# The third group of seven products moves to the last gate and up stage, and steps of sums are asked for at other places

## The chip, the cores and the metric

The kernel runs on one core of a Trainium2 chip. The metric is the time of one execution on the device in microseconds; the time before is 1002.94 us, the median of three runs (1001.95 to 1003.80).

## The reference, cut to what matters

Two layers over x of 256 positions by 1024 features, in float32. Each layer adds half a gated feed-forward, then a token mixer, then half of a second feed-forward:

```python
def swiglu(h, w_gate_up, w_down):
    a, b = jnp.split(h @ w_gate_up, 2, axis=-1)
    return (jax.nn.silu(a) * b) @ w_down

def hybrid_layer(x, ...):
    x = x + 0.5 * swiglu(rms_norm(x, ffn1_norm), ffn1_w_gate_up, ffn1_w_down)
    z = rms_norm(x, mix_norm) @ w_in
    u, q, k, v, gl = z[..., :o1], z[..., o1:o2], z[..., o2:o3], z[..., o3:o4], z[..., o4:]
    y_pool = multiscale_pool(u, pool_w, pool_scale)
    q = rope(rms_norm(q, q_norm)); k = rope(rms_norm(k, k_norm))
    y_attn = moba_attention(q, k, v)
    gates = jax.nn.sigmoid(gl + b_gate)
    x = x + (gates[0] * (y_pool @ w_branch_pool) + gates[1] * (y_attn @ w_branch_attn)) @ w_out
    x = x + 0.5 * swiglu(rms_norm(x, ffn2_norm), ffn2_w_gate_up, ffn2_w_down)
    return x
```

D is 1024, the feed-forward is 2816 wide (22 blocks of 128), and the mixer has 8 heads of 64. With 256 positions there is a single block of keys, so attention is causal within it.

## The kernel before, in words

**Units.** All weights lie in DRAM as units of 128 x 2048 float32, 1 MB each. `fetch` (line 143) has SyncE load one into a `raw` buffer (4 of them); ScalarE rounds it to `hi` (line 209) and VectorE takes the rest as `lo` (line 210), in two halves each. There is room for three units in parts, and `ahead` keeps what is split but not yet used. TensorE multiplies the parts with the parts of x (`hx`), all from the one helper at line 110. `plan` is the fixed order of the units.

**Stages.** The program runs six stages: layer 0's first feed-forward, its mix, its second feed-forward (base `FU`), layer 1's first (`LU`), its mix, and its second (`LU + FU`), the last. A feed-forward has a gate and up part (22 blocks), and a down part, whose 8 output columns are added to x.

**Groups in seven forms.** In the last three feed-forwards some of the blocks are not computed as wide pairs (`pair`, 32 matmuls each, one unit) but in groups of four blocks, by Strassen's and Winograd's scheme: seven products (`seven`, 16 matmuls each, one unit each) of forms of x and forms of the weights, and two turns (`turned`, four transposes each). Forms 1, 2 and 3 are quadrants of the weights; forms 4, 5, 6 and 7 are sums of quadrants. `FEED` says for each base which table gives the order: `TWO` has groups A and C (14 wide pairs, 14 products), `THREE` has A, B and C (10 wide pairs, 21 products). The forms of x (`x_forms`) are made at the head of each stage: all at once in `TWO`, one per entry of the table in `THREE`.

**Steps of sums.** The sums of quadrants are made ahead of time by DMAs from DRAM to DRAM, eight steps a group, 56 in all: a copy (`f7`, `f5` from the weights, `f6` from `f7`, `f4` from `f6`), and an accumulating DMA behind it. `far_sums` lists them in order, and each call of `go_on` has GpSimd issue the next one (line 183), behind the VectorE operation that was last marked when the call was made. An accumulating step waits for its copy to land, and a copy of a sum waits for that sum. GpSimd's queue is in order, so whatever stands behind a waiting step waits too; the only other work there is `pool_sums`, the pooling of the mix (lines 857 to 862), whose result VectorE reads in `pool_diff` (line 868), and one memset per mix (line 810). All DMAs share the 16 DMA engines: the loads go by SyncE's queue, the steps by GpSimd's.

**The end.** `add_x` ends each column of the down part. With `late_r` the factor r of the normalisation is applied to the column there (lines 674 to 676, and 681 and 682 for the very last column); without it, it has been applied to gate and up (line 468 in place of 465), and the last column needs line 684 alone. `late_r` is off in the last stage if that stage uses `TWO`.

Of the kernel before, what the change touches and what calls it, by code (L numbers as in the profile page):

```python
# [44 lines left out]
FU = NF + NF // 2 + 24  # L45
LU = FU + NF + NF // 2
# [7 lines left out]
TWO = (0, 1, "1A", 2, "2A", 3, 4, "7A", 5, "6A", 6, "5A", 7, "4A", "3A", 8, "t1A", "1C", (9, "t0A"), "2C", 10, "7C", 11, "6C",  # L54
       16, "5C", 17, "4C", "3C")
THREE = (0, 1, "1A", 2, "2A", "1B", 3, 4, "7A", "6A", 5, "5A", 6, "4A", "2B", "3A", "7B", "6B", 7, "t0A", "t1A", "5B",
         16, "1C", "4B", "3B", "6C", (17, "t0B"), "7C", "t1B", "5C", "2C", "3C", "4C")
FEED = {FU: TWO, LU: THREE, LU + FU: TWO}


def groups_of(base):
    return "AC" if FEED[base] is TWO else "ABC"


def feed_units(base):

    for n in FEED[base]:
        n = n[0] if isinstance(n, tuple) else n
# [6 lines left out]
C_G1, C_GM, C_G2, C_BG, C_PS, NG = 0, 8, 16, 24, 40, 44  # L75
# [3 lines left out]
def trunk_kernel(ctx: ExitStack, tc: tile.TileContext, x_in, w_in, pw_in, qkn_in, rope_in, mask_in, band_in, out):  # L79
    nc = tc.nc  # L80
# [47 lines left out]
    def unit():  # L128

        if not ahead:  # L130
            fetch()
        return ahead.pop(0)
# [17 lines left out]
    far, steps_left = {}, []  # L150

    def quadrant(base, g, q):

        n, kh = base + GROUPS[g] + (0 if q[1] == "1" else 2), int(q[0]) - 1
        return w_in[n:n + 2, :, kh * HALF:(kh + 1) * HALF].rearrange("u p c -> p u c")

    def two_rows(z):
        return z.rearrange("p (i c) -> p i c", i=2)

    def far_sums():  # L160

        rest = []
        for base in STAGES:
            for g in groups_of(base):
                one, two = ({z[0]: (base, g, z[0], z[i], kw) for z in SUMS}
                            for i, kw in ((1, {}), (2, {"accum_op": OP.add})))
                for z in one["7"], one["5"], two["7"]:
                    steps_left.append(z)
                    steps_left.extend(rest[:1])
                    rest = rest[1:]  # L170
                steps_left.extend((two["5"], one["6"]))
                rest = [two["6"], one["4"], two["4"]]
        steps_left.extend(rest)

    def go_on():

        if not steps_left:
            return
        base, g, f, src, kw = steps_left.pop(0)
        if not kw:  # L180
            far[f, g, base] = far_pool.tile([P, 2 * HALF], F32, name="f" + f, tag=f"{base}{g}{f}")
        src = two_rows(far[src, g, base]) if len(src) == 1 else quadrant(base, g, src)
        z = nc.gpsimd.dma_start(two_rows(far[f, g, base]), src, **kw)  # L183
        tc.add_manual_dep(z.ins, marks[-1].ins.name, mybir.DependencyInfo(
            mybir.DependencyClass.Sync, mybir.DependencyReason.DATA), reason="behind")
# [60 lines left out]
    def pair(w, t, other=None, at=0):  # L246

        ps = banks(pmm, "ps")
        columns(w, ps, range(at))
        if other:  # L250
            other()
        columns(w, ps, range(at, NK))
        drain(t, ps)
# [34 lines left out]
    x = gx[:, L * NG:L * NG + NK * S].rearrange("p (k s) -> p k s", s=S)  # L288
# [18 lines left out]
    for t in range(PAD - 1):  # L307
        g = min(g for g, w in enumerate(WINDOWS) if t < w - 1)
# [7 lines left out]
    def split_x(f, l, col):  # L316

        g = gain[:, l, col + f:col + f + 1]
        act(hx[:, f, 0, :], x[:, f, :], AF.Copy, scale=g)
        stt(hx[:, f, 1, :], x[:, f, :], g, hx[:, f, 0, :].bitcast(F32), op0=OP.mult, op1=OP.subtract)  # L320

    def square_x(f):

        if f == 0:
            act(acc, x[:, f, :], AF.Square)
        else:
            sq = small.tile([P, S], F32, name="sq", tag="sq", bufs=2)
            act(sq, x[:, f, :], AF.Square)
            tt(acc, acc, sq, op=OP.add)

    def prep(f, l, col):
        split_x(f, l, col)
        square_x(f)
# [83 lines left out]
    def bc2(a):  # L417
        return a.unsqueeze(1).to_broadcast([P, 2, a.shape[-1]])

    def ffn(after, n0=0, end=False, col=None, base=0, far_at=(), steps_at=()):  # L420
# [15 lines left out]
        abs_, more = {}, []  # L436
        late_r = not (end and FEED[base] is TWO)
        last = {}
# [38 lines left out]
        if n0:  # L477
# [6 lines left out]
            for i in range(n0 + 1, NF + 1):  # L484
                if i < NF:
                    pair(unit(), wide(i))
                    fetch()
                    if i >= 8 and i % 2 == 0:
                        go_on()
                if i == NF or i % 3 != 1:  # L490
                    for n in range(done, NF if i == NF else min(done + 2, i - 1), 2):
                        scaled = post(n)
                        done = n + 2
                        if i == n0 + 1:
                            behind(scaled, drained[-1])
        else:
# [11 lines left out]
            vt = acts.tile([P, 2, GW], F32, name="vt", tag="v")  # L508
            three = FEED[base] is THREE
            tk = {g: acts.tile([P, 2, GW], F32, name="tk", tag="tok", bufs=2) for g in ("AB" if three else "AC")}  # L510
# [113 lines left out]
            if three:  # L624
                go_on()
            for n in FEED[base][2:]:
                next(xf, None)
# [74 lines left out]
    def normed(pt, rt, name):  # L702
        z = acts.tile([P, 2, GW], F32, name=name, **({"tag": "v"} if name == "v" else {"tag": "tok", "bufs": 2}))
        for t in range(2):
            act(z[:, t, :], pt[:, t], AF.Copy, scale=rt[:, t:t + 1])
        return z
# [87 lines left out]
    def mix(l, after):  # L794
# [5 lines left out]
        pt = tokens()  # L800
        r = spread(*z)
        k = normed(pt, rt, "k")
        spare = acts.tile([P, 8 * GW], F32, name="spare", tag="ga")
        yk, pk = ([z[:, i] for i in range(4)] for z in (
            acts.tile([P, 4, 2, S], F32R, name=n, tag=t) for n, t in (("yk", "gc"), ("pk", "gd"))))
# [23 lines left out]
        def project_u():  # L829
            us = [unit() for _ in range(2)]  # L830
            for g in range(0, NW, 2):
                ps = banks(pmm, "ps")
                for k in range(NK):
                    for j in range(2):
                        chain(ps[:, j], *us[k // 4], k % 4 * 4 + g + j, hk[k], k == 0, k == NK - 1)
                z = uT[:, g:g + 2, PAD:]
                drain(z, ps)
                tt(z, z, bc2(r), op=OP.mult)

        pool = [gates[6 + g // 2][:, g % 2, :] for g in range(NW)]  # L840
        W = PAD + S
# [57 lines left out]
        rest = slice(3 * P, 4 * P)  # L899
# [45 lines left out]
        for h in range(NH):  # L945
            gate(h, *((lambda: score_two(h // 2), NK // 2) if h % 4 == 0 else ()))
            if h == 4:
                for p, y in enumerate(ys):
                    heads_end(p, y)
                known = soften_two()  # L950
            elif h < 2:
                soften(h)
            elif h % 4 == 2:
                turn_two(h // 4 * 2, (0, 1) if h > 4 else ())
            elif h == 3:
                pool_diff()
            open_gate(h)
            for _ in range(2 if h < 3 else 1):
                go_on()

        def branch(f, j, k0=0, k1=4):
# [40 lines left out]
        for f in range(4, NK):  # L1002
            if f % 2 == 0:
                ws.append(unit())
                go_on()
            for j in range(2):
                branch(f, j)
            if f == 5:
                fetch()
            mixed(f)  # L1010
        ws, sums = [], []

        def project(f, k0=0, k1=NK):
            if f % 2 == k0 == 0:
                ws.append(unit())
                go_on()
            if k0 == 0:
                sums.append(quarter("ps"))
            ps = sums[f][:, 0]
            chain3(ps, *ws[f // 2], f % 2 * 8 + k0, mk[k0:k1], k0 == 0, k1 == NK)  # L1020
            if k1 == NK:
                marks.append(tt(x[:, f, :], ps, x[:, f, :], op=OP.add))
                after(f)
# [4 lines left out]
    w3 = [buffers() for _ in range(3)]  # L1028
# [20 lines left out]
    for l in range(L):  # L1049
        l_of[0] = l  # L1050
        if l == 0:
            far_sums()
        ffn(lambda f: prep(f, l, C_GM), len(w3) if l == 0 else 0, col=C_G1, base=l * LU, far_at=(1, 3, 5, 7, 9), steps_at=(2,))
        if l == 0:
            for d, z in ((rope, rope_in), (mask, mask_in), (qkn, qkn_in)):
                nc.sync.dma_start(d, z)
        mix(l, lambda f: prep(f, l, C_G2))
        if l + 1 < L:
            ffn(lambda f: prep(f, l + 1, C_G1), col=C_G2, base=FU, far_at=(1, 3, 5, 7, 9), steps_at=(3, 6, 10, 16))
        else:  # L1060
            ffn(lambda f: nc.sync.dma_start(out[:, f, :], x[:, f, :]), end=True, col=C_G2, base=LU + FU)


# [88 lines left out]
```

## Time and profile before

| | |
|---|---|
| median of three runs | 1002.94 us |
| the profiled execution | 1001.16 us |
| its span, first to last instruction | 999.4 us |
| TensorE busy | 990.3 us (99%) |
| TensorE weight loads | 898.5 us (90%) |
| VectorE busy | 805.5 us (81%) |
| ScalarE busy | 654.9 us (66%) |
| GpSimd busy | 62.7 us (6%) |
| granted TensorE clock | 1.0 |
| moved by DMA | 273.65 MB, mean 274 GB/s |

Busy shares are of the span of one profiled execution; line numbers in the rows are those of the kernel before. In the rows PE is TensorE and PEld its weight loads, DVE is VectorE, ACT ScalarE, POOL GpSimd, and SP SyncE; a small q is the engine's queue. `raw<-w` is a weight load, `raw<-f` the load of a sum, and `f<-w` and `f<-f` are steps. `ps` are the sums of wide pairs, `b` those of products.

### The profile page before, as it was taken

How to read it: one execution, taken by the hardware profiler on the slowest of the kernel's cores; microseconds unless marked ns; L12 is line 12 of the kernel's file. 1: busy time of each engine (PE TensorE's matmuls, PEld its weight loads, DVE VectorE, ACT ScalarE, POOL GpSimd, SP SyncE). 2: the span in 40 equal slices, each digit the busy share in tenths (PEclk: the TensorE clock that was granted, in tenths of full speed). 3: DMA queues.
4: the chain of work that ended last, by engine and by line, in shares of the span. 5: the costliest groups of instructions: out<-in, count | busy, mean ns of one | idle time of the engine just before them, and what ended most of it. 6: DMA issues, size and time to landing. Idle time of an engine off the chain costs nothing.

```text
span 999.4 us, 16133 instructions
## 1 busy us (share of the span) xinstructions
PE 990.3 (99%) x6304; PEld 898.5 (90%) x6304; DVE 805.5 (81%) x1141; ACT 654.9 (66%) x981; POOL 62.7 (6%) x103
## 2 busy tenths in 40 slices
PE   9999999999999989999999999999999999999998
PEld 8988999998899978889898889988988998888898
DVE  6987767698788689887689998876988788988862
ACT  7856555567666587775568877555677568776641
POOL 0000001003101000000000000000130000000000
PEclk9999999999999999999999999999999999999999
DMA  8879899958999989898969989887878665787740
GB/s 295 315 269 274 312 317 266 318 194 252 281 345 313 341 311 318 330 323 331 306 216 297 340 293 324 323 288 247 229 250 296 192 213 211 255 285 260 252 148 22
DMA packets 47756, 273.65 MB, mean 274 GB/s; under 512 B 4576, under 2 KB 5856, under 8 KB 24928
## 3 DMA queue, kind: packets, MB, share of 16 engines
q1 hardware_dynamic: 35808, 213.90, 58.2%
q0 software_dynamic: 11872, 58.72, 23.9%
q8 instruction: 49, 0.80, 0.3%
q14 instruction: 27, 0.22, 0.1%
HBM read 271.56 MB, written 59.77 MB: 332 GB/s over the span
## 4 chain that ended last, share of the span: by engine, by line
PE 94%; DMA 2%; DVE 2%; ACT 1%; issue 0%; SPq 0%; ACTq 0%
PE ps L110 66%; PE b L110 13%; PE pt L110 7%; PE two L110 4%; DMA raw<-w 2%; PE pe L110 1%; PE sc L110 1%; DVE lo L210 1%; PE pt L780 1%; PE y L110 1%; PE b L588 0%; PE tp L736 0%; ACT pre L529 0%; PE pt L588 0%; ACT hi L209 0%
## 5 line engine op out<-in xcount | busy, mean ns | idle before, releaser
L210 DVE TENSOR_TENSOR lo<-raw,hi 128x1024 fp32r<-128x1024 f32 (+2 forms) x311 | 368.4, 1197 | 109.0 <-ACT hi L209 106.7
L209 ACT ACTIVATE hi<-raw 128x1024 fp32r<-128x1024 f32 (+2 forms) x311 | 318.4, 1033 | 202.7 <-PE ps L110 114.7
L110 PE MATMUL ps<-hx,hi 128*128 128x512 f32 x1248 | 423.4, 385 | 2.1 <-DVE ab L259 1.5
L110 PE MATMUL ps<-hx,lo 128*128 128x256 f32 x1248 | 341.8, 274 | 0.0
L110 PEld LDWEIGHTS ps<-hx,hi 128*128 128x128 f32 x1248 | 235.0, 188 | 44.8 <-DVE ab L259 1.8
L110 PEld LDWEIGHTS ps<-hx,lo 128*128 128x128 f32 x1248 | 235.3, 189 | 0.2 <-DVE lo L210 0.2
L199 DVE TENSOR_TENSOR lo<-raw,hi 128x1024 fp32r<-128x1024 f32 x98 | 118.5, 1221 | 26.0 <-ACT hi L198 25.7
L198 ACT ACTIVATE hi<-raw 128x1024 fp32r<-128x1024 f32 x98 | 102.9, 1055 | 49.8 <-PE ps L110 19.3
L110 PE MATMUL ps<-ga,hi 128*128 128x512 f32 (+1 forms) x264 | 87.8, 378 | 0.0
L110 PE MATMUL b<-hi,sf 128*128 128x512 f32 x224 | 76.6, 383 | 0.0
L110 PE MATMUL ps<-ga,lo 128*128 128x256 f32 x256 | 70.0, 273 | 0.0
L183 POOL DMA_DIRECT2D f<-w x42 | 39.3, 981 | 482.8 <-DVE ab L259 219.7
L110 PE MATMUL ps<-gb,hi 128*128 128x512 f32 (+1 forms) x198 | 65.4, 376 | 0.0
L110 PE MATMUL pt<-hi,hx 128*128 128x512 f32 x192 | 64.9, 384 | 0.0
L110 PE MATMUL b<-lo,sf 128*128 128x256 f32 x224 | 61.5, 275 | 2.5 <-DVE lo L199 2.5
L110 PEld LDWEIGHTS ps<-ga,hi 128*128 128x128 f32 x264 | 49.0, 188 | 8.2
L110 PE MATMUL pt<-lo,hx 128*128 128x256 f32 x192 | 52.5, 274 | 0.0
L110 PE MATMUL ps<-gb,lo 128*128 128x256 f32 x192 | 52.4, 273 | 0.0
L110 PE MATMUL b<-hi,hx 128*128 128x512 f32 x168 | 51.8, 388 | 0.0
L110 PEld LDWEIGHTS b<-hi,sf 128*128 128x128 f32 x224 | 42.0, 188 | 7.4
L110 PEld LDWEIGHTS ps<-ga,lo 128*128 128x128 f32 x256 | 48.1, 188 | 0.0
L110 PEld LDWEIGHTS b<-lo,sf 128*128 128x128 f32 x224 | 42.0, 188 | 2.8 <-DVE lo L199 2.8
(214 smaller groups left out, 1577.0 us busy)
## 6 DMA issues: line engine op xcount, KB each, us to landing
raw<-w SPq DMA_DIRECT2D x169, 1024.0 KB, 7.1
f<-w POOLq DMA_DIRECT2D x42, 1024.0 KB, 12.9
raw<-f SPq DMA_DIRECT2D x28, 1024.0 KB, 6.7
raw<-w SPq DMA_DIRECT2D x16, 256.0 KB, 5.4
out_dram<-gx SPq DMA_DIRECT2D x8, 128.0 KB, 1.9
gx<-x SPq DMA_DIRECT2D x3, 256.0 KB, 5.8
qk<-pw SPq DMA_DIRECT2D x2, 256.0 KB, 3.8
gx<-x SPq DMA_DIRECT2D x1, 300.0 KB, 2.9
```

Source lines behind the costliest of these rows:

```text
L110: return keep(nc.tensor.matmul(*args, **kw))
L183: z = nc.gpsimd.dma_start(two_rows(far[f, g, base]), src, **kw)
L198: act(hv, a, AF.Copy)
L199: tt(lv, a, hv.bitcast(F32), op=OP.subtract)
L209: act(hi, w, AF.Copy)
L210: return tt(lo, w, hi.bitcast(F32), op=OP.subtract)
L780: keep(nc.tensor.transpose(pt[:, h, o * P:(o + 1) * P], pr[:, h, c * P:(c + 1) * P], ident))
```

## The change

The table `THREE` goes from `LU` to `LU + FU`, and `TWO` from `LU + FU` to `LU`. `late_r` is thereby on in the last stage. `far_sums` now ends a stage's list before it begins the next one; before, the last three steps of a group were mixed with the first of the next group, across stages too. And `go_on` is called elsewhere:

```diff
-FEED = {FU: TWO, LU: THREE, LU + FU: TWO}
+FEED = {FU: TWO, LU: TWO, LU + FU: THREE}
...
 def far_sums():
-        rest = []
         for base in STAGES:
+            rest = []
             for g in groups_of(base):
...
-        steps_left.extend(rest)
+            steps_left.extend(rest)
...
-                    if i >= 8 and i % 2 == 0:
+                    if i in (8,11,14,17,19,21):
                         go_on()
...
         k = normed(pt, rt, "k")
+        go_on()
...
                 tt(z, z, bc2(r), op=OP.mult)
+                if g in (0,2):
+                    go_on()
...
             open_gate(h)
-            for _ in range(2 if h < 3 else 1):
+            if h in (0,2,3,4,5,6,7):
                 go_on()
...
                 ws.append(unit())
-                go_on()
+                if f in (6,):
+                    go_on()
...
                 ws.append(unit())
-                go_on()
+                if f in (4,):
+                    go_on()
...
-        ffn(..., base=l * LU, far_at=(1, 3, 5, 7, 9), steps_at=(2,))
+        ffn(..., base=l * LU, far_at=(1,3,5,7,9) if l else (1,3,5,7,9), steps_at=(6,11))
...
-            ffn(..., base=FU, far_at=(1, 3, 5, 7, 9), steps_at=(3, 6, 10, 16))
+            ffn(..., base=FU, far_at=(1,3,5,7,9), steps_at=(6,11))
...
-            ffn(..., end=True, col=C_G2, base=LU + FU)
+            ffn(..., end=True, col=C_G2, base=LU + FU, steps_at=(2,))
```

Counted from the code, the 56 steps are asked for so:

| stage | before | now |
|---|---|---|
| layer 0, first feed-forward | 12 | 11 |
| layer 0, mix | 20 | 15 |
| layer 0, second feed-forward (`FU`) | 9 | 7 |
| layer 1, first feed-forward (`LU`) | 7 | 7 |
| layer 1, mix | 8 | 15 |
| layer 1, second feed-forward (`LU + FU`) | 0 | 1 |

In layer 0's mix, 11 of the 20 stood at the gates, two at the branches and four at the output columns; of the 15 now, seven stand at the gates, one at the branches, one at the output columns, and two at the pooling's input.

GpSimd in layer 0's mix, from the last step ahead of the pooling sums on (`gates` and `spare` are written by the sums, `uT` is their input). Before:

```order
L183 DMA f6_1957<-w 256x1x1024
L858 TENSOR_TENSOR gates_2058<-uT_2056 128x256
L857 TENSOR_TENSOR spare_2051<-uT_2056 128x3x271
L857 TENSOR_TENSOR spare_2051<-spare_2051 128x2x269
L858 TENSOR_TENSOR gates_2058<-spare_2051 128x256 x2
```

Now:

```order
L183 DMA f4_2210<-f6_2049 16x16384
L861 TENSOR_TENSOR gates_2058<-uT_2056 128x256
L183 DMA f4_2210<-w 256x1x1024
L183 DMA f7_2316<-w 256x1x1024
L860 TENSOR_TENSOR spare_2051<-uT_2056 128x3x271
L860 TENSOR_TENSOR spare_2051<-spare_2051 128x2x269
L861 TENSOR_TENSOR gates_2058<-spare_2051 128x256 x2
```

Two steps stand between the first of the pooling sums and the others, and the first of them accumulates into the copy issued two rows above it, for whose landing it waits.

GpSimd in layer 1's mix, from the end of the pooling sums to the end of the program. Before:

```order
L862 TENSOR_TENSOR spare_7134<-spare_7134,uT_7139 128x64
L183 DMA f5_6835<-w 256x1x1024
L183 DMA f6_7501<-f7_6631 16x16384
L183 DMA f6_7501<-w 256x1x1024
L183 DMA f4_7566<-f6_7501 16x16384
L183 DMA f4_7566<-w 256x1x1024
```

Now:

```order
L865 TENSOR_TENSOR spare_7103<-spare_7103,uT_7108 128x64
L183 DMA f6_7330<-w 256x1x1024
L183 DMA f5_7600<-w 256x1x1024
L183 DMA f4_7655<-f6_7330 16x16384
L183 DMA f7_7368<-w 256x1x1024
L183 DMA f4_7655<-w 256x1x1024
L183 DMA f5_7600<-w 256x1x1024
L183 DMA f6_7930<-f7_7368 16x16384
L183 DMA f6_7930<-w 256x1x1024
L183 DMA f4_8382<-f6_7930 16x16384
L183 DMA f4_8382<-w 256x1x1024
```

Ten steps stand there in place of five: seven at the gates, one at the branches, one at the output columns, and the last one at the head of the last feed-forward.

SyncE's loads at the head of the last feed-forward (`w` of 128x2048 is a wide pair's unit, 128x2x1024 a quadrant, `f` a sum). Before:

```order
L193 DMA raw_8668<-w 128x2x1024
L143 DMA raw_8694<-w 128x2048
L193 DMA raw_8741<-w 128x2x1024
L143 DMA raw_8789<-w 128x2048
L143 DMA raw_8838<-w 128x2048
L193 DMA raw_8889<-f7_4798 128x2048
L143 DMA raw_8915<-w 128x2048
L193 DMA raw_8960<-f6_6534 128x2048
```

Now:

```order
L193 DMA raw_8648<-w 128x2x1024
L143 DMA raw_8674<-w 128x2048
L193 DMA raw_8721<-w 128x2x1024
L193 DMA raw_8759<-w 128x2x1024
L143 DMA raw_8793<-w 128x2048
L143 DMA raw_8841<-w 128x2048
L193 DMA raw_8896<-f7_5086 128x2048
L193 DMA raw_8922<-f6_6502 128x2048
L143 DMA raw_8948<-w 128x2048
```

A quadrant of the new group and the sum `f6` come earlier, so that two products follow each other without a wide pair between them, twice. Inside a stage of two or of three groups, the orders of TensorE, VectorE and ScalarE are those that such a stage had before.

More of the change, by code (lines that the diff above doesn't have):

```diff
@@ L1052, in trunk_kernel @@
             far_sums()
-        ffn(lambda f: prep(f, l, C_GM), len(w3) if l == 0 else 0, col=C_G1, base=l * LU, far_at=(1, 3, 5, 7, 9), steps_at=(2,))
+        ffn(lambda f: prep(f, l, C_GM), len(w3) if l == 0 else 0, col=C_G1, base=l * LU,
+            far_at=(1,3,5,7,9) if l else (1,3,5,7,9), steps_at=(6,11))
         if l == 0:
@@ L1058, in trunk_kernel @@
         if l + 1 < L:
-            ffn(lambda f: prep(f, l + 1, C_G1), col=C_G2, base=FU, far_at=(1, 3, 5, 7, 9), steps_at=(3, 6, 10, 16))
+            ffn(lambda f: prep(f, l + 1, C_G1), col=C_G2, base=FU, far_at=(1,3,5,7,9), steps_at=(6,11))
         else:
-            ffn(lambda f: nc.sync.dma_start(out[:, f, :], x[:, f, :]), end=True, col=C_G2, base=LU + FU)
+            ffn(lambda f: nc.sync.dma_start(out[:, f, :], x[:, f, :]), end=True, col=C_G2, base=LU + FU, steps_at=(2,))
 def _feat(a):
```

## The prediction, made before the change was run

> **What bounds the kernel now.** I read the page first, then the waits of TensorE, the chain of work, and last the stretches by window. The page's first part says how full each engine is:
>
> ```profile
> span 999.4 us, 16133 instructions
> ...
> PE 990.3 (99%) x6304; PEld 898.5 (90%) x6304; DVE 805.5 (81%) x1141; ACT 654.9 (66%) x981; POOL 62.7 (6%) x103
> ```
>
> TensorE is the bound, 9.1 us idle in a span of 999.4. A matmul busy for longer than it need be would hide in this figure, but the change removes or adds no matmul shape, so only the idle time can move. The waits of TensorE, whole span (waiter, releaser: us in total, times, longest):
>
> ```profile
> PE b L110 <- DVE lo L199: 2.5, 1, 2.5
> PE ps L110 <- DVE ab L259: 1.5, 1, 1.5
> PE busy L110 <- DVE eps L298: 1.1, 1, 1.1
> PE ps L110 <- ACT hi L209: 0.6, 1, 0.6
> ```
>
> The last two are the start of the program. The first two, 4.0 us, are the only waits in the middle, and both lie between 345 and 370 us, the head of layer 0's second feed-forward. The chain of waits shows what they hang on (start, us, what):
>
> ```profile
> 321.89 19.11 DMA raw<-w
> ...
> 341.37 1.06 ACT hi L198
> ...
> 356.68 3.22 ACT pre L529 x8
> ...
> 365.16 1.15 DVE lo L199
> 366.35 1.40 PE b L110 x7
> ```
>
> A 1 MB weight load took 19.11 us; ScalarE and VectorE, which split each load before TensorE can use it, ran late behind it and caught up only at 366. Why it took so long is in the windows of line 183, the steps of sums that GpSimd issues (POOL busy and count, clock, DMA share, GB/s):
>
> ```profile
> 240.00:290.00 50.00, 7.37 (x9) 1.00 0.97 300
> 290.00:345.00 55.00, 6.66 (x8) 1.00 1.03 322
> ...
> 514.00:560.00 46.00, 2.11 (x2) 1.00 0.92 293
> ...
> 735.00:790.00 55.00, 4.17 (x5) 1.00 0.80 249
> 790.00:830.00 40.00, 0.00 (x0) 1.00 0.63 211
> 830.00:870.00 40.00, 0.00 (x0) 1.00 0.64 237
> ```
>
> 17 steps were issued from 240 to 345, and the DMA engines were full. In the run-up to the last feed-forward (790 to 830) there was none. The DMA issues of three windows give the weight load's median landing time, first 290 to 345, then 514 to 560, then 790 to 830:
>
> ```profile
> raw<-w SPq DMA_DIRECT2D x8, 1024.0 KB, 16.1
> raw<-f SPq DMA_DIRECT2D x1, 1024.0 KB, 18.9
> ```
>
> ```profile
> raw<-w SPq DMA_DIRECT2D x6, 1024.0 KB, 7.3
> ```
>
> ```profile
> raw<-w SPq DMA_DIRECT2D x8, 1024.0 KB, 5.1
> ```
>
> So a load takes 5.1 us beside no step, 7.3 beside two, 16.1 beside eight. All busy times by window (PE, PEld, DVE, ACT, POOL, clock, DMA) show what each does to TensorE:
>
> ```profile
> 345.00:370.00 25.00, 20.98 (x124) 18.33 (x124) 22.44 (x35) 22.33 (x34) 0.50 (x1) 1.00 0.84 299
> 514.00:560.00 46.00, 46.00 (x278) 41.30 (x277) 43.61 (x57) 39.76 (x56) 2.11 (x2) 1.00 0.92 293
> ...
> 830.00:870.00 40.00, 40.00 (x242) 35.94 (x241) 38.23 (x51) 33.34 (x47) 0.00 (x0) 1.00 0.64 237
> ```
>
> Of the three heads of sevens, only the one behind the crowded mix leaves TensorE idle (25.00 - 20.98 = 4.0 us). The clock is full throughout.
>
> **The change, part by part.** *The third group moves.* It replaces four wide pairs by seven products and two turns. From the chain (a wide pair, a product, a turn):
>
> ```profile
> 517.58 2.72 PE b L110 x16
> 520.30 5.34 PE ps L110 x32
> ...
> 607.63 0.44 PE b L588 x4
> ```
>
> That is 4 x 5.34 = 21.4 us out and 7 x 2.72 + 2 x 0.44 = 19.9 in: 1.5 us less in the last feed-forward, 1.5 more in layer 1's first. The sum is nothing, as long as both heads stay fed. The order of VectorE, ScalarE and TensorE inside a stage of two or of three groups is unchanged; the last feed-forward now runs what the 514 to 560 row shows, where VectorE is 43.61 of 46.00 busy and TensorE did not wait. It hides the split work by only a little, so its cover is the speed of the loads: rival two prices that.
>
> *The end.* With three groups in the last stage the factor r comes in at line 672 and after, not at line 468. The last column of the output, at 996.08, was one VectorE operation behind the last matmul; now there are two:
>
> ```profile
> 996.08 0.42 DVE L684 SCALAR_TENSOR_TENSOR gx<-ps,gx 128x256 f32<-128x256 f32 x1 [6.19 <-PE ps L110]
> ```
>
> Nothing lies beside it, so it adds 0.4 us to the path. The other seven columns have their operations beside matmuls (the same row shows VectorE idle for 6.19 us): nothing. The halved scaling at line 465 in place of line 468 is VectorE time in the middle, hidden: nothing.
>
> *The steps.* Of line 183, over the span:
>
> ```profile
> L183 POOL DMA_DIRECT2D f<-w x42: 672/1049/1544, 59.4 to 769.9; - x42
> L183 POOL DMA_DIRECT2D f<-f x14: 502/519/993, 102.0 to 763.0; - x14
> ...
> DMA to landing us min/median/max: 5.4/12.3/28.8
> ```
>
> and the two queues (packets, MB, share of 16 engines):
>
> ```profile
> q1 hardware_dynamic: 35808, 213.90, 58.2%
> q0 software_dynamic: 11872, 58.72, 23.9%
> ```
>
> A step takes 0.239 x 999.4 / 56 = 4.27 us of all 16 engines. A 1.049 MB load takes 0.582 x 999.4 x 1.049 / 213.90 = 2.85 us. A wide pair uses a load every 5.34 us, 53% of the engines. From 240 to 345 the 17 steps want 72.6 us and some 18 loads 51 us: 124 us in 105, an overload of 19 us, of the size of that one late load. After the change (times of steps are my estimates, from where their marks stand before) layer 0's mix asks for two steps ahead of the pooling sums (about 233), seven at its gates (up to about 285), one at its sixth branch column and one at its fifth output column. From 230 to 290 that is 9 x 4.27 + 11 x 2.85 = 70 us in 60, still too much; from 290 to 345 it is 2 x 4.27 + 10 x 2.85 = 37 us in 55, so the 10 us carried over are gone by about 310. The head of the feed-forward then meets loads like those of the 514 or the 790 row, and the work of its head is the one that the 830 row shows without a wait. Gain: between 0 and the whole 4.0 us, taken as 4.0, since all three other rows (two, none, none) have TensorE without a wait.
>
> Layer 1's mix gets 15 steps for 8. Its gate stretch, 735 to 790, then holds seven for five: 7 x 4.27 + 9 x 2.85 = 56 us in 55, less than the 0.97 and 300 GB/s of the 240 to 290 row, during which no wait of TensorE is on the list. Behind it stand one step at about 797, one at about 818 and one at the head of the last stage. From 790 to 845: 3 x 4.27 + 14 x 2.85 = 53 us in 55. That is as tight as the 514 row (share 0.92), whose TensorE wait is zero: cost nothing, with rival two as the other end. The two feed-forwards lose three steps in all from their 21 and stay hidden.
>
> [...]
>
> Sum against the profiled execution: 1001.16 - 4.0 + 0.4 = 997.6. That execution was 1.78 under the median of the runs, 1002.94; against the median, -3.6 gives **999.3**.
>
> **Rivals.** *One: the stall is the work, not the loads.* In the chain, the 8.5 us from 356.68 to 365.16 are the forms of x (`pre`, `sf`, `vt`), and these stay. If they alone made the wait, 4.0 us stay and 0.4 comes on top: 1003.3, no change that can be told. Against it: the same work at 830 to 870, no wait. Chance 0.10.
>
> *Two: the stall moves to the last stage* (slower). There the three-group head uses 9 loads from 517.58 to 552.52, one per 3.88 us; the two-group head 8 loads in 32.2 us, one per 4.02:
>
> ```profile
> 552.52 2.69 PE b L110 x16
> ...
> 833.17 2.72 PE b L110 x16
> ...
> 865.36 5.35 PE ps L110 x32
> ```
>
> In the crowded window 9 loads were issued in 55 us, one per 6.1. The two-group head then lagged 8 x (6.1 - 4.02) = 16.6 us, of which 4.0 showed, so 12.6 are covered by loads held ahead. The three-group head would lag 9 x (6.1 - 3.88) = 20.0 and stall 7.4. Then 1002.94 - 3.6 + 7.4 = 1006.7. It outweighs the gain when loads come slower than one per 5.7 us between 790 and 845. For it: 15 steps in that mix, three of them late. Against it: three are not eight. Chance 0.08.
>
> *Three: the pooling sums come late.* Two steps now stand among GpSimd's pooling sums, and the first waits for a copy that was asked for two steps earlier. Now the sums run, and their result is used, at:
>
> ```profile
> 222.44 1.05 POOL L183 DMA_DIRECT2D f<-w  x1 [11.67 <-DVE k L730]
> ...
> 232.28 1.54 POOL L857 TENSOR_TENSOR spare<-uT 128x813 f32<-128x813 f32 x1 [6.18 <-PE ps L110]
> ...
> 238.89 0.32 POOL L862 TENSOR_TENSOR spare<-spare,uT 128x64 f32<-128x64 f32 x1
> ```
>
> ```profile
> 256.80 1.43 DVE L868 SCALAR_TENSOR_TENSOR uT<-gates,uT 128x256 f32<-128x256 f32 x4
> ```
>
> There are 17.6 us to spare. The copy is asked for where the 222.44 row now stands, at about 224, and lands within 12.3 us by the median: the sums end near 224 + 12.3 + 6.9 = 243. Only with the longest landing, 28.8, would they end at 224 + 28.8 + 6.9 = 259.7, 2.9 us late for VectorE. If all of that reached TensorE: 1002.2, no change that can be told. Chance 0.04.
>
> **How the numbers follow.** The forecast has 0.78. Its own range goes from 997.0 (the profiled time with the whole 4.0 gone and the end hidden, 997.2, rounded down) to 1000.8 (1.5 of the stall left). The runs before differ by 0.9 about their median, and 0.2%, 2.0 us, is about what a measurement of this kernel can tell from no change. Rivals one and three, 0.14, are no change; rival two, 0.08, is slower. To hold 8 in 10 the range goes up to rival three, 1002.3, and leaves out rivals one and two.
>
> **What would show it.** Right: the two waits of 2.5 and 1.5 us are off TensorE's list; loads in 290 to 345 land in under 9 us; the end shows two VectorE operations of 0.42 us behind the last matmul; the 735 to 790 window reads about 0.95 of DMA. Wrong: a wait `PE b <- DVE lo` at the head of layer 0's second feed-forward although loads there take 5 to 8 us (rival one); new waits from 840 to 880 with loads of over 12 us (rival two); a wait of VectorE line 871 on GpSimd (rival three).

## The result, and the profile after

The changed kernel took 996.01 us (median of 4 executions, 994.82 to 997.36) beside 1002.61 (4 executions) of the kernel before on the same chip: ratio 0.9933, 95% interval 0.9916 to 0.9951. The forecast was 3.6 us less and the result is 6.6 us less, 1.0 us below the range. The profiled execution took 995.49 us. The first lines of its page:

```profile
span 993.7 us, 16141 instructions
...
PE 988.1 (99%) x6304; PEld 897.2 (90%) x6304; DVE 805.0 (81%) x1149; ACT 656.8 (66%) x981; POOL 62.7 (6%) x103
```

TensorE's waits, whole span:

```profile
PE busy L110 <- DVE eps L298: 1.1, 1, 1.1
PE ps L110 <- ACT hi L209: 0.7, 1, 0.7
```

The two waits in the middle are gone; what is left is the start. The busy times by window (PE, PEld, DVE, ACT, POOL, clock, DMA share, GB/s) show where the crowd went:

```profile
290.00:345.00 55.00, 55.00 (x432) 53.12 (x431) 48.15 (x82) 36.10 (x55) 1.56 (x2) 1.00 0.75 248
345.00:370.00 25.00, 25.00 (x151) 22.46 (x150) 23.62 (x31) 22.27 (x35) 0.00 (x0) 1.00 0.60 223
735.00:790.00 55.00, 55.00 (x426) 51.14 (x425) 46.15 (x76) 38.76 (x73) 4.89 (x6) 1.00 0.97 297
790.00:845.00 55.00, 55.00 (x407) 52.15 (x406) 46.70 (x77) 39.35 (x63) 2.58 (x3) 1.00 0.85 269
```

Between 345 and 370 TensorE is busy for 25.00 of 25.00 us, where 20.98 stood before. The median landing times of the loads issued from 290 to 345, and below it from 790 to 845:

```profile
raw<-w SPq DMA_DIRECT2D x9, 1024.0 KB, 7.0
...
raw<-w SPq DMA_DIRECT2D x9, 1024.0 KB, 7.2
```

The first was 16.1 before. The next two fences cut both programs at the same matmuls (the first `ss` of a feed-forward, line 110): layer 0's second feed-forward up to the next, layer 1's first feed-forward and its mix, and the last stage up to the last matmul. Before:

```profile
335.53:514.08 178.55, 174.53 (x1049) 156.31 (x1047) 143.13 (x189) 118.69 (x166) 8.84 (x11) 1.00 0.92 313
514.08:829.67 315.59, 315.59 (x2078) 287.94 (x2077) 267.41 (x391) 218.10 (x336) 20.35 (x26) 1.00 0.82 271
829.67:996.05 166.38, 166.38 (x1022) 150.06 (x1020) 129.14 (x155) 104.58 (x139) 0.00 (x0) 1.00 0.59 208
```

After:

```profile
334.03:508.01 173.98, 173.98 (x1049) 156.31 (x1047) 143.47 (x189) 119.46 (x166) 5.85 (x7) 1.00 0.83 278
508.01:825.27 317.26, 317.26 (x2086) 289.42 (x2085) 262.93 (x386) 213.12 (x329) 25.64 (x33) 1.00 0.86 283
825.27:989.87 164.60, 164.60 (x1014) 148.54 (x1012) 132.42 (x167) 110.46 (x146) 1.03 (x1) 1.00 0.67 236
```

The stage of the stall is 4.57 us shorter; the group's move costs 1.67 in the second stretch and gives 1.78 back in the third. Behind the last matmul stand, in the timeline:

```profile
989.91 0.42 DVE L681 SCALAR_TENSOR_TENSOR t<-ps,r 128x256 f32<-128x256 f32 x1 [5.81 <-PE ps L110]
990.37 0.42 DVE L682 TENSOR_TENSOR gx<-gx,t 128x256 f32<-128x256 f32 x1
```

From the last matmul to the end of the span it is now 3.80 us, before 3.35. Together (-0.11 is 1.67 - 1.78, the group's move): -4.57 - 0.11 + 0.45 = -4.23. The two profiled executions differ by 5.67; 1.36 of the rest is the start, for the first of these `ss` of the whole program (layer 0's first feed-forward) stands at 30.39 us here and at 31.75 before. So 4.2 us are accounted for at places, and the 6.6 between the medians hold something that the two profiles do not.

### The profile page after: what moved, and what is told of

Its sections match the earlier page's. It is cut to its first block, busy times and chain, and to the rows that moved or that the text cites. A ratio compares the mean times of both kernels' runs of the same rounds, so it can differ in the third digit from the quotient of the medians.

```text
span 993.7 us, 16141 instructions
## 1 busy us (share of the span) xinstructions
PE 988.1 (99%) x6304; PEld 897.2 (90%) x6304; DVE 805.0 (81%) x1149; ACT 656.8 (66%) x981; POOL 62.7 (6%) x103
## 4 chain that ended last, share of the span: by engine, by line
PE 99%; DMA 0%; DVE 0%; ACT 0%; SPq 0%; issue 0%
PE ps L110 70%; PE b L110 13%; PE pt L110 7%; PE two L110 4%; PE pe L110 1%; PE sc L110 1%; PE pt L780 1%; PE y L110 1%; DMA raw<-w 0%; PE b L588 0%; PE tp L736 0%; PE pt L588 0%; PE st L110 0%; PE ss L110 0%; DVE t L681 0%; DVE gx L682 0%
## 5 line engine op out<-in xcount | busy, mean ns | idle before, releaser
L110 PE MATMUL ps<-gc,hi 128*128 128x512 f32 (+1 forms) x132 | 44.3, 376 | 0.0
```

Source lines behind the costliest of these rows:

```text
L110: return keep(nc.tensor.matmul(*args, **kw))
```

## The experiments

All ratios are to the kernel before, run beside each kernel on the same chip.

### Both kernels again

b_again1 is the kernel before and a_again the changed one, both without an edit.

> The kernel before, unchanged, taken again. Theory A (the time that the forecast lacks is in the size of the stall, which differs between executions, and in the first microseconds): its profile shows the two waits at the head of layer 0's second feed-forward, in a size other than 4.0 us, and the ratio is 1.000 within 0.1%. Theory B (the profiled execution was typical, and the missing 2 to 3 us of gain lie elsewhere): the waits are again 4.0 us within 0.5, and the start of the first full-speed matmul is within 0.2 us of that in the changed kernel's profile or not, by chance.

> The changed kernel, unchanged, taken again, on the same chip as the others of this call. Both theories: 0.9934 of the time before, within 0.002; no wait of TensorE behind the first 10 us in its profile. If the start differs by chance from execution to execution, its profile begins the first pe product anywhere between 9.0 and 10.5 us.

Measured: b_again1 1001.62 us, ratio 1.0004 (0.9991 to 1.0016); a_again 995.40, ratio 0.9952 (0.9936 to 0.9968). The gain is there again; the ratios of the two series make it 4.8 and 6.7 us. The waits of b_again1 at the head of layer 0's second feed-forward, and its stage from there to the next feed-forward:

```profile
PE b L110 <- DVE lo L199: 2.5, 1, 2.5
PE ps L110 <- DVE ab L259: 1.4, 1, 1.4
```

```profile
333.67:512.17 178.50, 174.54 (x1049) 156.34 (x1047) 143.22 (x189) 118.57 (x166) 8.85 (x11) 1.00 0.92 315
```

The stall is as large as in the first profile (3.9 us of waits beside 4.0, 178.50 us of stage beside 178.55), so theory A's first half, a stall of changing size, falls, and theory B's first half holds. In a_again the first `pe` product begins at 10.93 us, later than the 9.0 to 10.5 expected; what differs at the start is told at the end.

### The places in layer 0's mix put back

mix0_back is the changed kernel with layer 0's mix asking for steps where it did before:

```diff
-            if h in (0,2,3,4,5,6,7):
+            for _ in range((h != 1) if l else 2 if h < 3 else 1):
                 go_on()
...
-                if f in (6,):
+                if f in (6,) or not l:
                     go_on()
...
-                if f in (4,):
+                if f in (4,) or not l:
                     go_on()
```

and the three new calls ahead of the gates only for layer 1.

> The changed kernel with the places of layer 0's mix as before: 20 steps there, of which 17 behind the pooling sums. Theory A and my prediction's step (the crowd of steps in that mix makes the stall): the stall at the head of layer 0's second feed-forward is back at 4 us or more, loads from 290 to 345 us land in about 16 us, and the time is the time before plus 0.4: ratio 1.000, within 0.002. Rival (the move of the third group makes the gain): ratio 0.993.

Measured: 997.62 us, ratio 0.9968 (0.9957 to 0.9980), neither the 1.000 of the theory nor the 0.993 of the rival. A part of the stall returns. TensorE's wait behind the start, and then the loads issued from 290 to 345:

```profile
PE b L110 <- DVE lo L199: 1.2, 1, 1.2
```

```profile
raw<-w SPq DMA_DIRECT2D x9, 1024.0 KB, 14.3
```

The stage that took 178.55 before and 173.98 after takes 175.49 here. So the places of layer 0's mix bring back 1.5 of 4.57 us, not all. The sums are still asked for in the new list order and the first feed-forward still asks for one step less; in this profile two steps are in flight at 340 us where three were before. Which of the two keeps the other 3 us away was not tried.

### The group kept, the places changed

groups_kept has the group where it was before, and the new places:

```diff
-FEED = {FU: TWO, LU: TWO, LU + FU: THREE}
+FEED = {FU: TWO, LU: THREE, LU + FU: TWO}
...
-                    if i in (8,11,14,17,19,21):
+                    if i in (6,8,10,12,14,16,18,19,20,21):
                         go_on()
...
-            far_at=(1,3,5,7,9) if l else (1,3,5,7,9), steps_at=(6,11))
+            far_at=(1,3,5,7,9), steps_at=(2,5))
```

(the steps are asked for earlier since layer 1's first feed-forward needs its third group's sums).

> The groups stay as before (three in layer 1's first feed-forward, two in the last), the list ends stage by stage and the places are those of the changed kernel, with four more in the first feed-forward so that the sums are there in time. Theory A: no stall, and no second operation at the end: 0.4 us under the changed kernel, ratio 0.993. Rival (the group's move makes the gain): ratio 1.000.

Measured: 995.01 us, ratio 0.9942 (0.9925 to 0.9959). Its stages:

```profile
333.19:507.17 173.98, 173.98 (x1048) 156.31 (x1047) 143.58 (x189) 119.48 (x166) 5.88 (x7) 1.00 0.84 278
507.17:822.84 315.67, 315.67 (x2078) 287.88 (x2077) 268.35 (x391) 218.23 (x336) 23.96 (x30) 1.00 0.86 284
822.84:989.21 166.37, 166.37 (x1022) 150.04 (x1020) 129.12 (x155) 104.59 (x139) 0.00 (x0) 1.00 0.60 208
```

The first stage is the changed kernel's, the other two those of before. The move of the group brings nothing; the places of the steps, together with the new order of their list, which this kernel has too, bring all of it. What the order alone is worth was not tried.

### How many steps the run-up bears

Two kernels add steps to the changed one. tail_six asks at every branch and output column of layer 0's mix (six steps for two):

```diff
-                if f in (6,):
+                if f in (6,) or not l:
                     go_on()
...
-                if f in (4,):
+                if f in (4,) or not l:
                     go_on()
```

gates_eleven asks eleven times at layer 0's gates for seven:

```diff
-            if h in (0,2,3,4,5,6,7):
+            for _ in range((h != 1) if l else 2 if h < 3 else 1):
                 go_on()
```

> The changed kernel, with six steps of sums in place of two at the branch and output columns of layer 0's mix (300 to 345 us). Theory (the number of steps in flight there sets how late the loads are): loads in 290 to 345 take 10 to 19 us, a stall of 1 to 4 us comes back at the head of layer 0's second feed-forward, ratio to the kernel before 0.996 to 1.000, and some executions read a clock of 0.998. [...]

> The changed kernel with eleven steps of sums at the gates of layer 0's mix, as before, in place of seven, and the one at the branch columns and the one at the output columns kept as changed. With six steps at those columns and seven at the gates there was no stall; with eleven and six there was one of 1.4 us. Theory (the backlog from the gates and the steps at the columns add up): loads of 10 to 14 us up to 300 and of 5 to 10 us behind, no stall, ratio to the kernel before 0.993 to 0.995. Rival (the gates alone make the backlog that the stall comes from): loads of 15 us or more in 310 to 345 and a stall of 1 us or more, ratio 0.996 to 0.998.

Measured: tail_six 997.02 us, ratio 0.9941 (0.9928 to 0.9954); gates_eleven 995.76, ratio 0.9936 (0.9919 to 0.9953). Neither stalls; for gates_eleven that was expected. For tail_six, the stall that was expected did not come although its loads from 290 to 345 were late:

```profile
raw<-w SPq DMA_DIRECT2D x9, 1024.0 KB, 11.6
```

```profile
345.00:370.00 25.00, 25.00 (x152) 22.42 (x151) 23.68 (x31) 22.43 (x35) 0.00 (x0) 1.00 0.73 272
```

In gates_eleven, the loads, and then ScalarE's wait for a load from 290 to 370:

```profile
raw<-w SPq DMA_DIRECT2D x9, 1024.0 KB, 11.8
```

```profile
ACT hi L198 <- DMA raw<-w: 4.0, 1, 4.0
```

ScalarE waits 4.0 us there and TensorE not at all. The same wait in the kernel before, and in mix0_back:

```profile
ACT hi L198 <- DMA raw<-w: 8.8, 2, 5.5
```

```profile
ACT hi L198 <- DMA raw<-w: 6.5, 2, 3.9
```

So a median of 7.0, 11.6 and 11.8 us cost nothing, 14.3 cost 1.5 us and 16.1 cost 4.57. The trace of the changed kernel shows why: its loads for the head of the stage (issued 295 to 340) lie landed for 3 to 11 us until ScalarE takes them up, and the parts of those issued up to 330 lie ready for 5 to 9 us more before TensorE wants them. In mix0_back the first margin is 0.1 us for four loads of that stretch, and the second falls to 0.9.

### The steps of layer 1's mix asked for late

mix1_late puts eight of layer 1's steps just ahead of the last feed-forward:

```diff
-            if h in (0,2,3,4,5,6,7):
+            if h == 0 or (l == 0 and h in (2,3,4,5,6,7)):
                 go_on()
...
-                if f in (6,):
+                if f in (6,) or l:
                     go_on()
...
-                if f in (4,):
+                for _ in range(2 if l and f in (0, 2) else 1 if l or f == 4 else 0):
                     go_on()
```

> The changed kernel, with the steps of layer 1's mix asked for late: one at the gates in place of seven, eight at the branch and output columns in place of two, so that they are in flight from about 780 to 840 us, just ahead of the last feed-forward. Rival two of the prediction: loads of 12 us or more there, and the three-group head of the last stage stalls by 4 to 8 us, ratio to the kernel before 0.998 to 1.004. Theory as it now stands (a crowd costs about 1.5 to 4.6 us of stage time, as at the head of layer 0's second feed-forward): 1.5 to 5 us, ratio 0.996 to 1.000, a clock of 0.998 in some executions. If the head is covered by what is held ahead: no stall, ratio 0.995.

Measured: 995.87 us, ratio 0.9932 (0.9919 to 0.9944): no stall. Its windows, and the loads issued from 790 to 845:

```profile
735.00:790.00 55.00, 55.00 (x424) 51.11 (x423) 46.17 (x75) 39.00 (x72) 0.67 (x1) 1.00 0.55 184
790.00:845.00 55.00, 55.00 (x407) 52.18 (x406) 46.64 (x77) 39.22 (x63) 5.27 (x6) 1.00 1.02 333
```

```profile
raw<-w SPq DMA_DIRECT2D x9, 1024.0 KB, 11.1
raw<-f SPq DMA_DIRECT2D x2, 1024.0 KB, 11.5
```

The DMA engines were as full as in the crowd of before (1.02 beside 1.03), but for 55 us and not for 105, so loads still came one per 5.0 us (11 in 55). Of the eight late steps GpSimd issued six up to 811.4 us and two inside the last stage, at 830.7 and 845.8, since it waited for landings (16.3 us) and for VectorE in between. Rival two's own point was one load per 5.7, so its stall is neither shown nor excluded beyond that; these late steps are not enough for it.

### What the profiles of before did not show

Each execution comes with its mean granted clock. Of 67 executions of the kernel before in three series, 23 read 1.0 and took 1000.62 us in the mean, 44 read 0.998 or 0.997 and took 1002.38. The share is not the same in each series: 20 of 37, 11 of 13 and 13 of 17 read low. Of the 12 executions of the changed kernel none is below 0.999, nor is one of the 29 of groups_kept, tail_six, mix1_late, gates_eleven and one_op_end (told below); of mix0_back's 12 two are. A reading of 0.999 is the end of the program: in the trace of the changed kernel the clock falls at 992.4 us, behind the last matmul at 989.9, and in none of the fourteen traces does that take more than 0.9 thousandths off the mean (a_again). The profiled executions of before had so far read 1.0. b_again2 and b_again3 are the kernel before without an edit, profiled again.

> The kernel before, unchanged, one more profiled execution. Runs of it so far show a mean granted clock of 1.0 in some executions (about 1000.5 us) and of 0.998 in about half (about 1002 us); the two profiles of it both fell on 1.0. Theory (the stall sometimes makes the clock fall): if this execution reads 0.998, its clock column has a stretch of about 3.4 us well below 1.0 between 345 and 380 us, and that stage (second to third feed-forward's first wide pair, 178.5 us so far) takes 180 or more. Rival (the low reading is the start or the end of the program): with 0.998 the clock is full from 20 us to the last matmul, and the stage takes 178.5. If it reads 1.0, it tells nothing.

> The kernel before, unchanged, once more, with the same expectations as the run ahead of it: with a mean clock of 0.998, theory: a stretch of low clock of about 3.4 us between 345 and 380 us and that stage 180 us or more; rival: full clock there and 178.5 us.

Measured: b_again2 took 1000.87 us at 1.0, b_again3 1000.85 at 0.998. The windows of b_again3 around the first of its two waits, and its whole stage:

```profile
353.26:356.67 3.41, 1.49 (x10) 1.09 (x9) 3.15 (x5) 3.29 (x6) 0.00 (x0) 1.00 1.04 412
356.67:360.09 3.42, 3.42 (x13) 2.94 (x12) 2.79 (x5) 3.42 (x9) 0.00 (x0) 0.50 0.92 376
360.09:363.50 3.41, 3.41 (x21) 3.05 (x21) 3.41 (x7) 3.41 (x7) 0.00 (x0) 1.00 0.38 162
...
333.94:513.53 179.59, 176.46 (x1048) 157.70 (x1047) 143.46 (x190) 118.78 (x166) 8.84 (x11) 0.99 0.92 313
```

TensorE was busy for 1.49 of 3.41 us, and for the next 3.42 us the clock was 0.50: 13 matmuls where 21 fit into the stretch behind it. The stage took 179.59 us, a little under the 180 expected and 1.0 more than in the other profiles of this kernel (178.50 to 178.60); here the low stretch fell between the two waits, and the second wait shrank from 2.5 to 1.1 us, so part of its price was hidden. The borders can be counted. In the trace of the changed kernel the clock is full from 5.96 to 992.41 us and in that of the kernel before from 9.54 to 999.41, 289 and 290 stretches of 3.413. In b_again3 the first record of full clock stands at 5.10 us, and the low stretch begins 351.57 us behind it, 103 times 3.413. In pause_long (below) every change of the clock lies a whole number of such stretches behind the first record too, 43 for the first. Counted so from its own first record, at 6.95 us, the second wait of b_again2 lay across the border of two stretches:

```profile
361.94:365.35 3.41, 1.56 (x9) 1.11 (x8) 3.41 (x7) 3.41 (x7) 0.50 (x1) 1.00 0.30 125
365.35:368.76 3.41, 2.73 (x16) 2.48 (x17) 3.41 (x4) 3.41 (x6) 0.00 (x0) 1.00 0.91 310
```

1.56 of 3.41 busy, and the clock stayed full; it did so too in the first profile of this kernel, with 1.59 in the stretch from 364.53 to 367.94. Whether the clock fell at these waits thus went by how they lay in the stretches, whose borders lie otherwise in each execution, with a first record between 4.0 and 10.6 us. Of the 44 low executions only b_again3 was profiled; that the others lost their clock at the same place is inferred: in the four profiles of this kernel no other stretch between its start and its end has TensorE busy for under 3.0 of 3.41 us.

### Pauses without transfers

To part the idle time from the crowded DMA engines, pause_long adds six pauses of TensorE to the down part of layer 0's first feed-forward of the changed kernel; it computes six sums that nobody reads:

```diff
                 add_x(f, ps, f < NK - 1 or not end, r[0] if late_r else None)
+                if not base and 0 < f < NK - 1:
+                    mm(quarter("pz")[:, 0, :1], lhsT=x[:, f, :P], rhs=ones[:, :1], start=True, stop=True)
```

pause_brief has the same matmul read `t` behind `add_x`'s first operation.

> The changed kernel with six pauses of TensorE added in the down part of layer 0's first feed-forward: behind each of the columns 1 to 6, one matmul of 128x1 reads the finished column of x, so TensorE waits until ScalarE and VectorE have added the last column. From the rows there each pause should be 2 to 3.5 us, 12 to 21 us in all, about 7.5 us apart. No transfer is added. Theory (an idle stretch of TensorE that fills more than about half of one of the 3.4 us stretches in which the granted clock is set makes the clock fall to a half for the next one, at some 1.7 us): two to five of the six pauses are followed by a low stretch, the mean clock reads 0.991 to 0.997, and the time rises by 3 to 9 us beyond the pauses. Rival (the clock fell in the kernel before because of the crowded DMA engines, not the idle time): clock as in the changed kernel, 0.999 to 1.0, and the pauses alone are added.

> The same six places, but the added matmul reads the column's copy right behind ScalarE's first operation, so each pause should be 0.6 to 1.5 us, 4 to 9 us in all. Theory (the clock falls only where more than about half of a 3.4 us stretch is idle): no low stretch or one, mean clock 0.998 to 1.0, and the time rises by the pauses alone. Rival (any interruption can make it fall): several low stretches here too, clock 0.997 or less.

Measured: pause_long 1023.28 us, ratio 1.0209 (1.0186 to 1.0232), clock 0.988 to 0.992; pause_brief 1002.89, ratio 1.0008 (0.9997 to 1.0019), clock 0.999 or 1.0. Two pauses of pause_long with the stretch behind each, and the whole stage and mix:

```profile
149.52:152.93 3.41, 1.40 (x9) 1.31 (x10) 2.66 (x6) 0.82 (x2) 0.50 (x1) 1.00 0.58 195
152.93:156.34 3.41, 3.41 (x12) 2.89 (x11) 0.48 (x1) 1.06 (x1) 0.00 (x0) 0.50 1.23 485
173.41:176.82 3.41, 1.65 (x10) 1.22 (x9) 2.46 (x4) 1.07 (x2) 0.00 (x0) 1.00 0.87 305
176.82:180.23 3.41, 3.27 (x20) 2.99 (x21) 1.98 (x4) 1.88 (x3) 1.06 (x1) 1.00 0.42 38
...
29.98:360.18 330.20, 313.96 (x2014) 284.69 (x2013) 244.12 (x361) 190.94 (x294) 28.78 (x37) 0.97 0.82 263
```

The same stretch of pause_brief, and of the changed kernel:

```profile
29.94:340.82 310.88, 306.66 (x2014) 278.65 (x2013) 243.72 (x361) 190.40 (x294) 28.78 (x37) 1.00 0.87 279
```

```profile
30.39:334.03 303.64, 303.64 (x2003) 277.34 (x2001) 243.38 (x361) 190.40 (x294) 28.79 (x37) 1.00 0.88 286
```

Four of the six long pauses were followed by a low stretch, one of them by two in a row; none of the brief ones was. TensorE's busy time rose by 313.96 - 306.66 = 7.30 us for five low stretches, 1.46 us each, beside the 16.24 us of idle time. Busy 1.40 of 3.41 let the clock fall, 1.65 did not, and with b_again3 and b_again2 what let it fall and what did not lie as close as 1.49 and 1.56 us busy, 44 and 46%. Ahead of b_again3's low stretch the DMA engines were full (1.04), ahead of pause_long's first at 0.58, while at 0.87 and 1.65 us busy the clock stayed; and the pauses came with no transfer of their own: it is the idle time that made the clock fall. Beyond its idle time pause_long's stage is 313.96 - 303.64 = 10.32 us longer, over the 3 to 9 expected, since the pauses have a second price: each of pause_brief's six idles 4.22 / 6 = 0.70 us, and the stage is 7.24 us longer, so TensorE's busy time is 306.66 - 303.64 = 3.02 us more, 0.5 for each pause with its added matmul.

### One operation at the end

one_op_end is the changed kernel with the factor r applied at gate and up in the last stage too:

```diff
-        late_r = not (end and FEED[base] is TWO)
+        late_r = not end
```

> The changed kernel, with the factor r of the last stage applied at gate and up, as a stage with two groups had it, so that one VectorE operation in place of two stands behind the last matmul. By the prediction's end term: 0.4 us between the last matmul and the end of the span less than in the changed kernel (3.35 in place of 3.80), the scaling of gate and up hidden, ratio to the kernel before 0.4 thousandths below the changed kernel's, which the times alone can't tell. Rival: the wider scalings cost VectorE time that the three-group head does not have; that stage (164.60 us to the last matmul) gets longer by more than 0.4 us.

Measured: 994.68 us, ratio 0.9927 (0.9910 to 0.9943). The last stage, and what is behind its last matmul:

```profile
826.67:991.27 164.60, 164.60 (x1014) 148.53 (x1012) 132.70 (x160) 110.27 (x146) 1.03 (x1) 1.00 0.67 236
```

```profile
991.31 0.42 DVE L684 SCALAR_TENSOR_TENSOR gx<-ps,gx 128x256 f32<-128x256 f32 x1 [6.20 <-PE ps L110]
```

The stage is as long as the changed kernel's, and the span ends 3.35 us behind the last matmul, 0.45 less. Of all kernels run this has the lowest median; that it beats the changed kernel is shown by the rows, not by the times, whose intervals overlap.

## Why the prediction was right in direction and wrong in size

**The stall.** That TensorE's two waits hang on the crowd of steps was right: without the crowd they are gone, with the group kept they are gone too, and with the places put back a part returns. Rival one falls: the forms of x are unchanged and TensorE does not wait.

**The step that failed** is "Gain: between 0 and the whole 4.0 us". The idle time was taken as the most that the stall can cost, with the reason "so only the idle time can move"; the lower end of the range, 997.0, rests on the same 4.0. The stall cost more in two ways. First, the stage is 4.57 us shorter, of which 178.55 - 174.53 = 4.02 was idle and 0.55 was the same 1049 matmuls taking longer (174.53 us busy for 173.98); mix0_back, with one wait in place of two, has half of that (0.27: 175.49 of stage, 1.51 more than the changed kernel's, for 1.24 of idle time). Second, "the clock is full throughout" was true of the profiled execution alone. In 44 of 67 executions of the kernel before the mean clock was low, and these took 1002.38 - 1000.62 = 1.76 us longer: 44/67 x 1.76 = 1.16 us in the mean. b_again3 shows one such stretch, and the pauses show that idle time made it. The changed kernel has no idle stretch behind its start, and none of its 12 executions reads below 0.999.

The offset of 1.78 us between the profiled execution and the median was carried to the changed kernel as if it were chance. In the 67 executions 1.16 us of such an offset is this term, which the change takes away with the stall; the clocks of the four executions of the first comparison are not on record.

With both, the sum is -4.57 - 0.11 + 0.45 - 1.16 = -5.4, which takes 1002.61 to 997.2, just inside the forecast's range. The means over all executions with a recorded clock, 1001.78 for the kernel before (67) and 996.13 for the changed one (12), differ by 5.65, but were not all taken on the same chips; in the series of b_again1 and a_again, on one chip, the gain is 4.8, with an interval of 3.2 to 6.4. The 6.6 of the first comparison has an interval of 4.9 to 8.4 and holds all of these. What is between 5.4 and 6.6, and so what took the result below 997.0, is not settled; the start varies by up to 2.6 us from execution to execution in both kernels (below), and 4 executions of each do not average that out.

**The single step in the run-up.** Beside the single step in flight from 317.3 to 328.4 the load issued at 320.4 took 11.0 us, more than the 7.3 beside two steps in the profile of before and less than the 16.1 beside eight, and the load issued at 316.0 took 4.8. No stall was kept, since the parts of the slowest one were ready 5.7 us early. The forecast of "under 9 us" for the loads there was wrong for this one and one other (9.4), and right for their median of 7.0; that the whole 4.0 us of idle time would go was right.

**The group, the end, the mixes.** The group's move gave -0.11 us for 0, and the two operations at the end cost 0.45 for 0.4. Layer 1's mix with 15 steps cost nothing, at a DMA share of 0.97 in 735 to 790 for the 0.95 forecast. The prediction's own sum for that stretch, 56 us in 55, is a share of 1.02 and not "less than the 0.97" beside which it stands; and its sum for 790 to 845 counted 14 loads, where 11 were issued. Rival two did not come: 7.2 us for a load ahead of the last stage, and no wait of TensorE in that stage even in mix1_late. Rival three did not come: the step among the sums waited 2.1 us for its copy, up to 227.09, the sums' last operation ended at 238.3 and VectorE read them at 255.9.

## What to carry to other kernels

A wait of the bounding engine is priced by the length of its stage between two fixed instructions, not by its idle time, and where that engine's clock follows its use (here 0.50 for 3.42 us behind a wait, in b_again3), by several executions with their clocks: a profile at full clock may stand for a third of them, as here (23 of 67). Late transfers cost nothing here while one of two margins held, the time for which a landed buffer lies (3 to 11 us in the changed kernel, 0.1 in mix0_back) and the time for which its product lies (5 to 9, and 0.9); in mix0_back they cost 1.5 us. Read both per buffer before forecasting a stall or its end. When a profiled execution differs from the median, ask what the difference is before carrying it along.

## What the runs showed of the hardware that was not expected

Ahead of the end of the program the granted clock fell to 0.50, in the traces, for a whole stretch of 3.41 us behind one in which TensorE was busy for 1.11 to 1.49 us (1.92 idle in the latter; four such in pause_long, one in b_again3), it stayed full behind 1.56, 1.59 and 1.65 (b_again2, the first profile of before, pause_long), and it did not come back behind a low stretch with 1.54 us idle in it (pause_long, 163.17 to 166.58, followed by another low one). At the start the clock came to full at another time in each execution. From 6.0 to 9.5 us, behind the first record of full clock in the changed kernel's trace (5.96) and ahead of it in that of before (9.54), 19 matmuls began in the one and 11 in the other. In the same time there were 22 in groups_kept,

```profile
6.00:9.50 3.50, 3.50 (x22) 3.10 (x21) 2.72 (x8) 3.11 (x9) 0.00 (x0) 1.00 0.99 324
```

and 11 in a_again:

```profile
6.00:9.50 3.50, 3.50 (x11) 2.94 (x12) 3.11 (x10) 3.38 (x11) 0.00 (x0) 1.00 1.00 360
```

The clock column prints 1.00 in both, since the profile has no record ahead of the first change; only the count of matmuls tells. Over the profiled executions the first record of full clock lies between 4.0 and 10.6 us, and the first feed-forward's `ss` between 29.6 and 32.3.
